# Regrouping the high and low parts of split fp32 products, with weight lows, latent casts and mixing work moved

## The chip, the cores and the metric

The kernel runs on one core of a Trainium2 chip. The metric is the device time of one execution in microseconds. TensorE (PE) multiplies matrices into PSUM, whose eight banks hold 512 fp32 columns each in this kernel; VectorE (DVE), ScalarE (ACT) and GpSimd (POOL) work beside it; SyncE (SP) issues most of the DMAs.

## The reference

Two layers over 512 latent and 256 context tokens (768 in all, six blocks of 128), width 1024, in fp32. Each layer is a half-step SwiGLU FFN, a token mixer, and a second FFN; each of these three is modulated (shift, scale, gate) and closed by a layer norm of the residual sum. The mixer of layer 0 is a chunked gMLP, that of layer 1 is grouped-query attention. The last FFN runs for the latent tokens alone.

```python
def swiglu(h, w_in, w_out):
    g, u = jnp.split(h @ w_in, 2, axis=-1)
    return (jax.nn.silu(g) * u) @ w_out

def ffn_sublayer(x, shift, scale, gate, w_in, w_out, ln_g, ln_b):
    y = swiglu(modulate(x, shift, scale), w_in, w_out)
    return layer_norm(ALPHA * x + 0.5 * gate * y, ln_g, ln_b)

def gmlp_mix(h, w_in, sgu_g, sgu_b, w_s, b_s, w_out):
    b_, t_, _ = h.shape
    u, v = jnp.split(jax.nn.gelu(h @ w_in, approximate=False), 2, axis=-1)
    v = layer_norm(v, sgu_g, sgu_b)
    v = v.reshape(b_, t_ // CHUNK, CHUNK, GMLP_GROUPS, GMLP_HALF // GMLP_GROUPS)
    v = jnp.einsum('gpq,bnqgc->bnpgc', w_s, v) + b_s.T[None, None, :, :, None]
    return (u * v.reshape(b_, t_, GMLP_HALF)) @ w_out

def attend(q, k, v):
    ...
    s = jnp.einsum('bkgqd,bktd->bkgqt', qg, k, preferred_element_type=jnp.float32) * (hd ** -0.5)
    p = jax.nn.softmax(s, axis=-1)
    o = jnp.einsum('bkgqt,bktd->bkgqd', p.astype(v.dtype), v)
```

D_FF is 2816, the gMLP's half width 3072 in 8 groups, chunks have 128 tokens, and there are 8 query heads and 2 key/value heads of 128.

## The kernel before, in words

**Split products.** TensorE multiplies in a shortened fp32 form ("fp32r"). To keep fp32's precision each operand is split into a high part, which ScalarE casts, and a low part, which VectorE makes by subtracting the high part from the operand. A product is then the sum of high by high, high by low and low by high. In `product()` a weight tile `w` (128x512: four pieces of the contraction, `k`) meets a combination `c` of the activations h: twelve matmuls of 128x384, three for each `k`, in the order high-high, high(w)-low(c), low(w)-high(c). `pair_step()` does this for the latent FFN with two times 256 columns. In the gMLP's v a step takes four weights and runs nine matmuls of 128x512 with each, on three PSUM banks, one for each block of tokens; the step's banks are evacuated after the fourth weight. Attention's scores and values are split alike.

**Strassen.** The large products run by a Strassen scheme of two by two blocks, whose right operands are combinations of h (B11, B21, T1 to T4, B22). They are made step by step in the generators `combine()` and `combine_latent()`: VectorE's subtractions `zraw`, `q` and `t`, ScalarE's casts into `comb`, VectorE's low parts of `comb`. `slot()` stands between products: it flushes the pending low parts of weights (`flush()`), takes further weights (`pump()`: each a ScalarE cast now and a VectorE low part that is put off to the next flush), evacuates the finished bank and takes one step of the combining.

**Weights.** SP's queue loads raw tiles of 256 KB into six buffers; some are summed with others for Strassen; the eight `w` buffers hold high and low side by side. The instructions of each engine keep the program's order around all of this, so what is written first is issued first.

**Fillers.** The modulation vectors of later sub-layers are made in between: VectorE multiplies tiles `mraw` of w_mod into `acc` (SCALAR_TENSOR_TENSOR acc<-mraw), and GpSimd reduces them over the partitions. `fill_pair()` issues one filler, or two where only one condition is left (`light`), as in ffn(1,0). GpSimd's queue also carries the activations' spill and return (act<-stage, q<-act).

**Order of the work.** ffn(0,0), gMLP, ffn(0,1), ffn(1,0), attention, latent ffn(1,1). In the gMLP, the spatial mixing of v runs between the products of u: for each of 24 pieces `j` six matmuls of 128x128 (`ps<-zraw,v`), three to a bank in columns 0 to 383, on two banks from a rotation of four (`mix_bank()`); every three pieces, the next group's spatial weight is transposed (`ps<-ident,s`) and summed with a matmul of ones, each in a bank that it takes from the same rotation. VectorE's `S` operations read the banks.

At the end of attention `close()` runs the last block's out-projection in two halves; between them `after(half)` releases four weights and pumps the next four, which are the latent FFN's first. VectorE then makes gate, sum, statistics and `nb`, with which ScalarE normalises `z`.

In the profile nearly every instruction has line 92, that of the wrapper which keeps program order.

Of the kernel before, what the change touches and what calls it, by code (L numbers as in the profile page):

```python
# [13 lines left out]
P = 128  # L14
# [49 lines left out]
OPEN_LAT = [(0, 0), (1, 0), (0, 1), (2, 0), (1, 1), (3, 0), (2, 1), (4, 0), (3, 1), (4, 1)]  # L64

# [31 lines left out]
class Backbone:  # L97
# [707 lines left out]
    def combine(self):  # L805


        sub = lambda out, a, b: self.dve.tensor_tensor(out, a, b, ALU.subtract)
# [80 lines left out]
    def combine_latent(self):  # L889

        N = self.ht // P
        sub = lambda out, a, b: self.dve.tensor_tensor(out, a, b, ALU.subtract)
# [134 lines left out]
    def out_proj(self, acts, l, i, factor, end, prev, gate_at=2):  # L1027
# [9 lines left out]
        for half, order in enumerate(orders):  # L1037
            body = n - CLOSE * half
            for x in range(body):
# [28 lines left out]
                elif residual and x > 2 and (half or x % 2):  # L1068
                    residual.pop(0)()
                    self.fill(int(self.light))  # L1070
                elif half or x < n - 1:
                    self.fill_pair()
                    if prev is None and x % 8 == 3:
                        self.fill()
# [100 lines left out]
    def product(self, ps, name, go_on=False):  # L1175
# [5 lines left out]
        for k in range(4):  # L1181
            s = slice(k * P, k * P + P)
            first, last = not go_on and k == 0, k == 3
            kw = dict(skip_group_check=True) if go_on else {}
            self.mm(ps, w[:, 0, s], c[:, 0, k], first, False, **kw)
            self.mm(ps, w[:, 0, s], c[:, 1, k], False, False, **kw)
            self.mm(ps, w[:, 1, s], c[:, 0, k], False, last, **kw)
# [137 lines left out]
    def pair_step(self, ps, name, go_on, early=None, post=lambda: None):  # L1325

        for x in range(2):
# [5 lines left out]
            for k in range(4):  # L1333
                s = slice(k * P, k * P + P)
                self.mm(o, w[:, 0, s], c[:, 0, k], not go_on and not x and k == 0, False, **kw)
                self.mm(o, w[:, 0, s], c[:, 1, k], False, False, **kw)
                self.mm(o, w[:, 1, s], c[:, 0, k], False, k == 3, **kw)
# [137 lines left out]
    def gmlp_v(self, room, spill, vst):  # L1475
# [43 lines left out]
        def step(x, name, go_on, evacuate):  # L1519
            kw = dict(skip_group_check=True) if go_on else {}  # L1520
            for k in range(4):
# [4 lines left out]
                for t in range(HALF):  # L1526
                    ps, s = sets[x][t], slice(t * P, t * P + P)
                    self.mm(ps, c[:, 0, k, s], w[:, 0], not go_on and k == 0, False, **kw)
                    self.mm(ps, c[:, 0, k, s], w[:, 1], False, False, **kw)
                    self.mm(ps, c[:, 1, k, s], w[:, 0], False, k == 3, **kw)  # L1530
# [86 lines left out]
    def gmlp(self, l, i, nblocks, end, prev):  # L1617
# [30 lines left out]

        def group(g):
# [6 lines left out]
            act.copy(wT, ps[:, 0:P])  # L1656
            yield
            ps = mix_bank()
            self.mm(ps[:, 0:P], self.ones, wT, True, True)
            dve.tensor_copy(r, ps[:, 0:P])  # L1660
# [30 lines left out]
        def spatial(j):  # L1691
# [4 lines left out]
            self.grp_next = next(self.following)  # L1696
            if j % 3 == 2:
                load_ws(j // 3 + 2)
            v = ring[:, j % 4]
            banks = [mix_bank(), mix_bank()]  # L1700
            for b in range(NB):
                o = (b % HALF) * P
                self.mm(banks[b // HALF][:, o : o + P], v[:, b], wT, True, True)
            fetches.append([2, j + 4])
# [162 lines left out]
    def attention(self, l, i, nblocks, end, prev):  # L1867
# [71 lines left out]
        def scores(n):  # L1939
# [4 lines left out]
            for c in (slice(0, 512), slice(512, TOK)):  # L1944
                self.mm(sc[:, c], qh, k[:, 0, c], True, False)
                self.mm(sc[:, c], qh, k[:, 1, c], False, False)
                self.mm(sc[:, c], ql, k[:, 0, c], False, True)
# [29 lines left out]
        def values(pr):  # L1977
# [3 lines left out]
            for t0, t1 in ((0, 3), (3, NB)):  # L1981
                for t in range(t0, t1):
                    ph, pl = [pT[pr % 2][:, x, t] for x in range(2)]
                    self.mm(po, v[:, 0, t], ph, t == 0, False)
                    self.mm(po, v[:, 0, t], pl, False, False)
                    self.mm(po, v[:, 1, t], ph, False, t == NB - 1)
# [96 lines left out]
        def closing(b):  # L2083
# [461 lines left out]
```

## Time and profile before

| | |
|---|---|
| median of 3 runs | 2770.55 us (2768.8 to 2772.38) |
| profiled execution | 2770.93 us |
| its span, first to last instruction | 2769.1 us |
| mean granted TensorE clock | 0.996 |
| busy: TensorE, VectorE, ScalarE, GpSimd | 2716.4, 2139.0, 1377.7, 675.0 us |
| matmuls | 14930 |
| read from and written to HBM | 401.75 and 65.77 MB, 169 GB/s |

Rows of the timeline read: start and length in us, engine, line, operation, tiles written and read, shape, and in brackets the idle time ahead of it and what ended that. The ends of matmuls are modelled, so a matmul's length (about 0.39 us for 512 columns) is longer than the distance from one start to the next; a row of several matmuls shows that distance as the difference between two rows' lengths, divided by the difference of their counts.

### The profile page before, as it was taken

The numbers are of one execution on the slowest core, as the hardware profiler recorded it, in microseconds if no ns is written. First come the engines' busy times: TensorE is split into PE (matmuls) and PEld (weight loads), VectorE is DVE, ScalarE is ACT, GpSimd is POOL, SyncE is SP. The second block draws the span as 40 slices with busy tenths as digits, with TensorE's granted clock in tenths as the row PEclk, the third lists the DMA queues.
The fourth block names the chain that finished last, engine by engine and source line by source line (L and its number), as shares of the span: only waits on it lengthen the run. The fifth ranks groups of instructions, "written<-read, shape, count | busy, mean of one in ns | idle before, by whom it ended". The sixth has DMA issues, their size and how long they took to land.

```text
span 2769.1 us, 42794 instructions
## 1 busy us (share of the span) xinstructions
PE 2716.4 (98%) x14930; PEld 2480.4 (90%) x14930; DVE 2139.0 (77%) x3724; ACT 1377.7 (50%) x2755; POOL 675.0 (24%) x829
## 2 busy tenths in 40 slices
PE   7999999999999999999999999999999999999998
PEld 5999987888899988899998889999888888899987
DVE  6878878487789977687887659788785698787766
ACT  7544433475666632654444246444432666665532
POOL 1003255312122344100325130024342121122121
PEclk9999999999999999999999999999999999999999
DMA  7444566367656674344547534455594524489673
GB/s 236 143 138 139 145 222 220 104 212 233 202 178 190 210 259 139 120 150 142 145 135 236 163 106 145 142 148 142 173 311 146 149 69 87 127 209 216 164 234 133
DMA packets 442896, 468.15 MB, mean 169 GB/s; under 512 B 30840, under 2 KB 323128, under 8 KB 442680
## 3 DMA queue, kind: packets, MB, share of 16 engines
q1 hardware_dynamic: 393592, 343.00, 40.7%
q0 software_dynamic: 49088, 122.42, 15.4%
q8 instruction: 117, 1.92, 0.3%
q14 instruction: 99, 0.81, 0.1%
HBM read 401.75 MB, written 65.77 MB: 169 GB/s over the span
## 4 chain that ended last, share of the span: by engine, by line
PE 57%; DVE 4%; ACT 3%; issue 2%; DMA 2%; POOL 1%; SPq 0%; DVEq 0%; ACTq 0%; POOLq 0%
PE ps L92 56%; DMA raw<-in_ffn_w_in_dram 1%; DVE w L92 1%; PE pp L92 1%; ACT h L763 0%; DVE q L92 0%; ACT z L2443 0%; POOL acc L542 0%; ACT w L92 0%; ACT p L1957 0%; DVE stage L92 0%; DMA mraw<-in_w_mod_dram 0%; DMA raw<-in_gmlp_w_in_dram 0%; DVE z L92 0%; DVE nm L1949 0%
## 5 line engine op out<-in xcount | busy, mean ns | idle before, releaser
L92 PE MATMUL ps<-comb,w 128*128 128x384 f32 (+1 forms) x8400 | 1381.0, 324 | 11.9 <-DVE w L92 3.7
L92 PEld LDWEIGHTS ps<-comb,w 128*128 128x128 f32 x8400 | 1361.0, 189 | 20.1 <-DVE w L92 7.1
L92 PE MATMUL ps<-w,acts 128*128 128x512 f32 (+1 forms) x3792 | 863.8, 389 | 4.7 <-DVE q L92 4.1
L92 PEld LDWEIGHTS ps<-w,acts 128*128 128x128 f32 x3792 | 707.8, 188 | 152.5 <-DVE q L92 4.9
L92 ACT CAST w<-raw 128x512 fp32r<-128x512 f32 x655 | 401.8, 622 | 486.0 <-PE ps L92 369.9
L92 DVE TENSOR_TENSOR w<-raw,w 128x512 fp32r<-128x512 f32 x655 | 455.0, 702 | 240.2 <-ACT w L92 237.8
L542 POOL PARTITION_ALL_REDUCE acc<-acc x224 | 294.2, 1385 | 276.5 <-DVE acc L92 248.5
L92 DVE SCALAR_TENSOR_TENSOR acc<-mraw,cs,acc 128x512 f32<-128x512 f32 x392 | 284.8, 760 | 42.4 <-DMA mraw<-in_w_mod_dram 42.1
L92 ACT COPY q<-ps 128x384 f32<-128x384 f32 (+1 forms) x248 | 122.0, 493 | 266.4 <-PE ps L92 262.6
L92 POOL DMA_DIRECT2D act<-stage x92 | 57.6, 675 | 780.5 <-DVE stage L92 734.3
L92 DVE TENSOR_TENSOR w<-sums,w 128x512 fp32r<-128x512 f32 x278 | 191.3, 696 | 59.4 <-ACT w L92 58.4
L92 POOL DMA_DIRECT2D q<-act x240 | 135.4, 621 | 320.3 <-DVE acts L92 180.0
L92 ACT CAST w<-sums 128x512 fp32r<-128x512 f32 x278 | 171.6, 621 | 57.4 <-DVE sums L92 30.3
L92 DVE TENSOR_TENSOR acts<-q,acts 128x384 fp32r<-128x384 f32 (+2 forms) x278 | 153.0, 589 | 31.2 <-ACT acts L92 31.1
L92 PE MATMUL ps<-w,comb 128*128 128x512 f32 x756 | 173.6, 390 | 1.4 <-ACT ps L92 1.0
L92 ACT CAST acts<-q 128x384 fp32r<-128x384 f32 (+2 forms) x278 | 132.8, 512 | 77.6 <-DMA q<-act 60.2
L92 PEld LDWEIGHTS ps<-w,comb 128*128 128x128 f32 x756 | 141.3, 188 | 32.3 <-ACT ps L92 1.7
L206 POOL TENSOR_TENSOR rs<-ve,mhalf 128x1 f32<-128x1 f32 (+3 forms) x47 | 38.2, 812 | 262.8 <-DVE ve L203 167.2
L92 ACT ACTIVATE q<-q 128x384 f32<-128x384 f32 (+1 forms) x94 | 51.2, 554 | 82.4 <-DVE q L92 82.2
L346 DVE TENSOR_TENSOR sums<-raw 128x512 f32<-128x512 f32 x78 | 55.4, 710 | 31.0 <-DMA raw<-in_gmlp_w_in_dram 18.3
L92 PE MATMUL ps<-w,h 128*128 128x512 f32 x336 | 77.9, 391 | 0.0
L92 ACT COPY ps<-ps 128x384 f32<-128x384 f32 (+1 forms) x60 | 28.5, 475 | 98.1 <-PE ps L92 97.9
(200 smaller groups left out, 2485.6 us busy)
## 6 DMA issues: line engine op xcount, KB each, us to landing
raw<-in_ffn_w_in_dram SPq DMA_DIRECT2D x420, 256.0 KB
mraw<-in_w_mod_dram SPq DMA_DIRECT2D x256, 256.0 KB
raw<-in_ffn_w_out_dram SPq DMA_DIRECT2D x176, 256.0 KB
q<-act POOLq DMA_DIRECT2D x224, 192.0 KB, 4.3
raw<-in_gmlp_w_in_dram SPq DMA_DIRECT2D x132, 256.0 KB
act<-stage POOLq DMA_DIRECT2D x76, 384.0 KB, 3.2
zhat<-z POOLq DMA_DIRECT2D x26, 512.0 KB, 3.0
raw<-in_gmlp_w_out_dram SPq DMA_DIRECT2D x48, 256.0 KB
```

The source lines that it names most:

```text
L92: return self.tc.keep_in_program_order(f(*args, **kwargs))
L206: self.last_rstd = self.nc.gpsimd.tensor_tensor(rs, ve, self.mhalf[:, 0:1].to_broadcast([P, n]), ALU.pow).ins
L346: dve.tensor_tensor(s1, u1, u2, ALU.add)
L542: nc.gpsimd.partition_all_reduce(part, part, P, bass_isa.ReduceOp.add)
```

## The change

It has five parts, each of them a change of order; the number of instructions of each kind stays the same.

1. In `product()`, `pair_step()`, the gMLP's v, attention's scores and its values, all high-high matmuls come first, then those with the low part of the activations, then those with the low part of the weights. The low part of `w` is wanted by the ninth of twelve matmuls, before by the third (in v by the seventh of nine, before by the second); that of `c` by the fifth, before by the second.
2. In `combine()` and `combine_latent()` the function `sub` flushes the pending weight lows right behind each subtraction.
3. In the out-projection of a light FFN (ffn(1,0)) the pair of fillers after the first step of the first half is left out there, and comes a step later.
4. In the spatial mixing the group's transposition and ones matmul use columns 384 to 511 of the second bank of the piece that has just been multiplied, and come behind its six matmuls.
5. At the end of attention `after()` also pumps behind the second half, with low parts put into free slots of VectorE's order at once (`slots`), so that four more weights are cast and lowered before the last block is closed.

```diff
+PARTS = (0, 0), (0, 1), (1, 0)
...
     def combine(self):
-        sub = lambda out, a, b: self.dve.tensor_tensor(out, a, b, ALU.subtract)
+        def sub(out, a, b):
+            self.dve.tensor_tensor(out, a, b, ALU.subtract)
+            self.flush()
...
-                elif half or x < n - 1:
+                elif half or x < n - 1 and (x or not self.light):
                     self.fill_pair()
...
         c = self.comb[name]
-        for k in range(4):
-            s = slice(k * P, k * P + P)
-            first, last = not go_on and k == 0, k == 3
-            kw = dict(skip_group_check=True) if go_on else {}
-            self.mm(ps, w[:, 0, s], c[:, 0, k], first, False, **kw)
-            self.mm(ps, w[:, 0, s], c[:, 1, k], False, False, **kw)
-            self.mm(ps, w[:, 1, s], c[:, 0, k], False, last, **kw)
+        kw = dict(skip_group_check=True) if go_on else {}
+        for n, (x, y) in enumerate(PARTS):
+            for k in range(4):
+                s = slice(k * P, k * P + P)
+                first, last = not go_on and n == 0 and k == 0, n == 2 and k == 3
+                self.mm(ps, w[:, x, s], c[:, y, k], first, last, **kw)
...
-                for t in range(HALF):
-                    ps, s = sets[x][t], slice(t * P, t * P + P)
-                    self.mm(ps, c[:, 0, k, s], w[:, 0], not go_on and k == 0, False, **kw)
-                    self.mm(ps, c[:, 0, k, s], w[:, 1], False, False, **kw)
-                    self.mm(ps, c[:, 1, k, s], w[:, 0], False, k == 3, **kw)
+                for n, (i, j) in enumerate(PARTS):
+                    for t in range(HALF):
+                        s = slice(t * P, t * P + P)
+                        first, last = not go_on and n == 0 and k == 0, n == 2 and k == 3
+                        self.mm(sets[x][t], c[:, j, k, s], w[:, i], first, last, **kw)
...
+        beside = []
+        def spare():
+            return beside.pop() if beside else mix_bank()[:, 0:P]
...
-            ps = mix_bank()
-            self.tp(ps[:, 0:P], ws_raw.pop(g))
+            ps = spare()
+            self.tp(ps, ws_raw.pop(g))
...
-            self.grp_next = next(self.following)
...
             for b in range(NB):
                 o = (b % HALF) * P
                 self.mm(banks[b // HALF][:, o : o + P], v[:, b], wT, True, True)
+            beside[:] = [banks[1][:, HT : HT + P]]
+            self.grp_next = next(self.following)
...
                 def after(half):
                     self.release(4)
-                    if not half:
-                        self.pump()
+                    self.slots = bool(half)
+                    self.pump()
+                    self.slots = False
```

What this does to the order of the instructions is shown at three places. In the rows, numbers tell tiles apart.

VectorE at the opening of ffn(1,0): `w` rows are weight lows, `zraw`, `q` and `t4` the subtractions, `comb` the low part of a combination. Before:

```order
L92 TENSOR_TENSOR zraw_16424<-z_14840,h32_16097 128x512
L92 TENSOR_TENSOR q_16426<-z_14840,zraw_16424 128x512
L92 TENSOR_TENSOR w_16418<-raw_16017,w_16418 128x512
L92 TENSOR_TENSOR t4_16449<-h32_16097,q_16426 128x512
L92 TENSOR_TENSOR comb_16423<-q_16426,comb_16423 128x4x128
L92 TENSOR_SCALAR z_14840<-ps_16457,modA_16089,modB_16090 128x128 x4
L92 TENSOR_TENSOR w_16444<-raw_16045,w_16444 128x512
```

After:

```order
L94 TENSOR_TENSOR zraw_16410<-z_14826,h32_16083 128x512
L94 TENSOR_TENSOR w_16404<-raw_16003,w_16404 128x512
L94 TENSOR_TENSOR q_16413<-z_14826,zraw_16410 128x512
L94 TENSOR_TENSOR t4_16435<-h32_16083,q_16413 128x512
L94 TENSOR_TENSOR w_16430<-raw_16031,w_16430 128x512
L94 TENSOR_TENSOR comb_16409<-q_16413,comb_16409 128x4x128
```

The first low part moved ahead of q, the second ahead of comb's low part and of the four TENSOR_SCALAR.

TensorE where the spatial mixing meets the preparation of a group. Before:

```order
L92 MATMUL ps_7247<-comb_6029,w_7191 128x384 x12
L92 MATMUL ps_7411<-zraw_7295,v_5589 128x128 x3
L92 MATMUL ps_7412<-zraw_7295,v_5589 128x128 x3
L92 MATMUL ps_7423<-ident_69,s512_7240 128x128
L92 MATMUL ps_7427<-zraw_7295,v_5589 128x128 x3
L92 MATMUL ps_7428<-zraw_7295,v_5589 128x128 x3
L92 MATMUL ps_7436<-comb_5305,w_7200 128x384 x12
```

After:

```order
L94 MATMUL ps_7247<-comb_6029,w_7191 128x384 x12
L94 MATMUL ps_7410<-zraw_7295,v_5589 128x128 x3
L94 MATMUL ps_7411<-zraw_7295,v_5589 128x128 x3
L94 MATMUL ps_7423<-zraw_7295,v_5589 128x128 x3
L94 MATMUL ps_7424<-zraw_7295,v_5589 128x128 x3
L94 MATMUL ps_7424<-ident_69,s512_7240 128x128
L94 MATMUL ps_7435<-comb_5305,w_7200 128x384 x12
```

The transposition stands behind the second piece, and writes the bank that this piece has written.

VectorE where the last block of attention is closed (gate into `q`, sum into `z`, statistics, `ve1`, `nb`). Before:

```order
L176 TENSOR_TENSOR w_23941<-raw_23503,w_23941 128x512
L988 SCALAR_TENSOR_TENSOR q_23963<-ps_23913,gate_22895 128x512
L999 TENSOR_TENSOR z_23697<-z_23697,q_23963 128x512
L1004 BN_STATS st_23702<-z_23697 128x6
L965 BN_AGGR mv_23967<-st_23702 128x2
L203 TENSOR_SCALAR ve1_23969<-mv_23967 128x1
L970 SCALAR_TENSOR_TENSOR nb_23973<-mv_23967,rs1_23970 128x1
```

After:

```order
L178 TENSOR_TENSOR w_23927<-raw_23489,w_23927 128x512
L998 SCALAR_TENSOR_TENSOR q_23965<-ps_23899,gate_22881 128x512
L178 TENSOR_TENSOR w_23944<-raw_23567,w_23944 128x512
L1009 TENSOR_TENSOR z_23683<-z_23683,q_23965 128x512
L178 TENSOR_TENSOR w_23948<-raw_23572,w_23948 128x512
L1014 BN_STATS st_23688<-z_23683 128x6
L178 TENSOR_TENSOR w_23952<-raw_23915,w_23952 128x512
L975 BN_AGGR mv_23969<-st_23688 128x2
L178 TENSOR_TENSOR w_23956<-raw_23920,w_23956 128x512
L205 TENSOR_SCALAR ve1_23971<-mv_23969 128x1
L980 SCALAR_TENSOR_TENSOR nb_23975<-mv_23969,rs1_23972 128x1
```

Four weight lows, which stood behind `nb` before, stand between its operations.

More of the change, by code (lines that the diff above doesn't have):

```diff
@@ L891, in combine_latent, with sub @@
         N = self.ht // P
-        sub = lambda out, a, b: self.dve.tensor_tensor(out, a, b, ALU.subtract)
+        def sub(out, a, b):
+            self.dve.tensor_tensor(out, a, b, ALU.subtract)
+            self.flush()
         cut = lambda t: t[:, :].rearrange("p (k t) -> p k t", t=P)
@@ L1332, in pair_step @@
             c, o = self.comb[name], ps[:, x * self.ht : x * self.ht + self.ht]
[L1333 to L1337, printed above, removed]
+            for n, (i, j) in enumerate(PARTS):
+                for k in range(4):
+                    s = slice(k * P, k * P + P)
+                    first, last = not go_on and not x and n == 0 and k == 0, n == 2 and k == 3
+                    self.mm(o, w[:, i, s], c[:, j, k], first, last, **kw)
         self.slot(post, 4, 0, early)
@@ L1525, in step @@
                 c = self.comb[name]
-                for t in range(HALF):
-                    ps, s = sets[x][t], slice(t * P, t * P + P)
-                    self.mm(ps, c[:, 0, k, s], w[:, 0], not go_on and k == 0, False, **kw)
-                    self.mm(ps, c[:, 0, k, s], w[:, 1], False, False, **kw)
-                    self.mm(ps, c[:, 1, k, s], w[:, 0], False, k == 3, **kw)
+                for n, (i, j) in enumerate(PARTS):
+                    for t in range(HALF):
+                        s = slice(t * P, t * P + P)
+                        first, last = not go_on and n == 0 and k == 0, n == 2 and k == 3
+                        self.mm(sets[x][t], c[:, j, k, s], w[:, i], first, last, **kw)
                 if k == 3:
@@ L1652, in group @@
             yield
-            ps = mix_bank()
-            self.tp(ps[:, 0:P], ws_raw.pop(g))
+            ps = spare()
+            self.tp(ps, ws_raw.pop(g))
             wT = self.zplace()[:, 0:P]
-            act.copy(wT, ps[:, 0:P])
+            act.copy(wT, ps)
             yield
-            ps = mix_bank()
-            self.mm(ps[:, 0:P], self.ones, wT, True, True)
-            dve.tensor_copy(r, ps[:, 0:P])
+            ps = spare()
+            self.mm(ps, self.ones, wT, True, True)
+            dve.tensor_copy(r, ps)
             yield wT, r, bs
@@ L1695, in spatial @@
             wT, r, bs = self.grp
-            self.grp_next = next(self.following)
-            if j % 3 == 2:
-                load_ws(j // 3 + 2)
             v = ring[:, j % 4]
@@ L1703, in spatial @@
                 self.mm(banks[b // HALF][:, o : o + P], v[:, b], wT, True, True)
+            beside[:] = [banks[1][:, HT : HT + P]]
+            self.grp_next = next(self.following)
+            if j % 3 == 2:
+                load_ws(j // 3 + 2)
             fetches.append([2, j + 4])
@@ L1943, in scores @@
             sc = self.pair()
[L1944 to L1947, printed above, removed]
+            for m, (x, y) in enumerate(PARTS):
+                for c in (slice(0, 512), slice(512, TOK)):
+                    self.mm(sc[:, c], (qh, ql)[x], k[:, y, c], m == 0, m == 2)
             nm = self.sm([1], "nm")
@@ L1981, in values @@
             for t0, t1 in ((0, 3), (3, NB)):
[L1982 to L1986, printed above, removed]
+                for n, (x, y) in enumerate(PARTS):
+                    for t in range(t0, t1):
+                        self.mm(po, v[:, y, t], pT[pr % 2][:, x, t], n == 0 and t == 0, n == 2 and t == NB - 1)
                 if t1 < NB:
```

## The prediction

> **What bounds the kernel now.** I read the page's busy times first, then who TensorE waits for, then TensorE's timeline wherever a wait stood.
>
> ```profile
> span 2769.1 us, 42794 instructions
> PE 2716.4 (98%) x14930; PEld 2480.4 (90%) x14930; DVE 2139.0 (77%) x3724; ACT 1377.7 (50%) x2755; POOL 675.0 (24%) x829
> PE ps L92 <- DVE w L176: 4.4, 11, 1.0
> PE ps L92 <- DVE w L92: 4.0, 9, 0.7
> ```
>
> TensorE is busy for 98% of the span, so the kernel is TensorE's stream plus 52.7 us of its gaps. The change leaves the number of matmuls as it is; it can win only at gaps, and at the slow stretches that follow some of them. The two last rows are the gaps that a weight's low part ends: 8.4 us in all, much of it at the start, in matmuls outside the products.
>
> **The openings of the two light FFNs, ffn(0,1) and ffn(1,0).** TensorE, VectorE and ScalarE at the second of them, and the weight loads' wait from 1100 to 1400 us:
>
> ```profile
> 1667.52 2.70 PE L92 MATMUL ps<-comb,w 128*128 128x384 f32 x14
> 1670.76 2.35 PE L92 MATMUL ps<-comb,w 128*128 128x384 f32 x12 [0.55 <-DVE w L92]
> 1673.84 0.44 PE L92 MATMUL ps<-comb,w 128*128 128x384 f32 x1 [0.73 <-DVE w L92]
> 1670.02 0.68 DVE L92 TENSOR_TENSOR w<-raw,w 128x512 fp32r<-128x512 f32 x1
> 1670.66 0.62 ACT L92 CAST w<-raw 128x512 fp32r<-128x512 f32 x1
> PEld ps L92 <- DVE w L92: 1.9, 2, 1.0
> ```
>
> Fourteen matmuls take 2.70 us and twelve 2.35, so one costs 0.175. After fourteen from 1667.52 the next was due at 1669.97 and came at 1670.76, 0.8 late; twelve from there were due to end at 1672.86, and the next came at 1673.84, 1.0 late. Both times two matmuls of a product had run and the third wanted the low part. In the new order the low part is wanted by the ninth, six matmuls (1.05 us) later, and VectorE makes it one subtraction (0.6 us) earlier. That covers both lags. What is late next is the second weight's cast: ScalarE's cast of h's combination waits for q, which now stands behind the low part, so the cast at 1670.66 moves 0.6 later and ends near 1671.9, where its product is due at about 1671.7: 0.2 lost of 1.8. From 1100 to 1400 the last row shows the same two waits at ffn(0,1) (they are the only ones there). Gain 1.65 twice, **+3.3** (0 if VectorE is late all the same, up to 3.6).
>
> **Two single starts.** The first product of the first FFN, and the first weight of the gMLP's v; the last row is the group of all v's matmuls:
>
> ```profile
> 48.62 0.62 PE L92 MATMUL ps<-comb,w 128*128 128x384 f32 x2 [1.89 <-ACT w L175]
> 49.69 3.52 PE L92 MATMUL ps<-comb,w 128*128 128x384 f32 x10 [0.45 <-DVE w L176]
> 562.64 0.49 PE L92 MATMUL ps<-w,comb 128*128 128x512 f32 x1 [0.19 <-ACT w L92]
> 563.37 2.12 PE L92 MATMUL ps<-w,comb 128*128 128x512 f32 x8 [0.23 <-DVE w L92]
> L92 PE MATMUL ps<-w,comb 128*128 128x512 f32 x756 | 173.6, 390 | 1.4 <-ACT ps L92 1.0
> ```
>
> At 48.62 two matmuls should take 0.35 and took 1.07: 0.7 goes; the wait for ScalarE ahead stays, and so does the half-speed stretch behind it (ten matmuls in 3.52). At 562.64 one matmul took 0.73 where 0.23 is due: 0.5 goes. **+1.2** (0.5 to 1.7).
>
> **Spatial mixing.** TensorE at its two long waits, and a stretch of the span with the granted clock in the next to last column group (time, TensorE busy, clock, DMA share, GB/s):
>
> ```profile
> 748.82 0.83 PE L92 MATMUL ps<-zraw,v 128*128 128x128 f32 x6
> 751.61 0.91 PE L92 MATMUL ps<-zraw,v 128*128 128x128 f32 x6 [1.95 <-DVE S L92]
> 752.76:756.17 3.41, 3.41 (x13) 0.50 0.59 168
> 750.84 1.14 DVE L92 SCALAR_TENSOR_TENSOR S<-ps,sguT,s 128x384 f32<-128x384 f32 x2
> 929.34 0.83 PE L92 MATMUL ps<-zraw,v 128*128 128x128 f32 x6
> 931.61 0.91 PE L92 MATMUL ps<-zraw,v 128*128 128x128 f32 x6 [1.43 <-DVE S L92]
> ```
>
> Here the group's transposition or its ones matmul takes a bank of its own out of the rotation of four, so a second spatial step comes back to a bank that the step before it still has in use, and waits for VectorE. With that work in the spare columns each step takes exactly two banks and meets those of two steps ago. Six matmuls from 748.82 end their issue near 749.5; the next came at 751.61: 2.1. From 929.34: 1.6. The first wait is followed by 3.41 us at half the granted clock, in which 1.7 us of matmuls are lost. **+5.4** (3.5 if the half-clock stretch stays or falls elsewhere; 5.5).
>
> The trace granted half the clock after an idle time of 1.95 us. The Trainium skill, "TensorE: Matmul & The Clock Gate", section "Why this matters for your kernels", warns only of idle gaps above about 3 us. By that rule the 1.7 us here would have another cause and stay, and the new 2 us waits below could not halve the clock; the sum would be 2761.5 instead of 2760.7. The row decides.
>
> **The gMLP's v, where the new order costs.** A step takes four weights, and with each runs nine matmuls on the same three banks; 756 / 36 = 21 steps. Before, three matmuls run on each bank in turn; after, every matmul changes the bank. TensorE, ScalarE's evacuations, the weight loads, and a stretch with the clock:
>
> ```profile
> 687.62 3.79 PE L92 MATMUL ps<-w,comb 128*128 128x512 f32 x16
> 692.41 1.88 PE L92 MATMUL ps<-w,comb 128*128 128x512 f32 x7 [1.00 <-ACT ps L92]
> 691.76 0.59 ACT L92 COPY ps<-first 128x512 f32<-128x512 f32 x1 [0.83 <-DVE q L92]
> 649.66 0.59 ACT L92 COPY ps<-v 128x512 f32<-128x512 f32 x1
> 650.30 0.76 PEld L92 LDWEIGHTS ps<-w,comb 128*128 128x128 f32 x4 [0.25 <-ACT ps L92]
> 687.00:690.40 3.40, 3.40 (x17) 1.00 0.70 260
> ```
>
> One matmul costs (3.79 - 0.39) / 15 = 0.227 us. The step's third bank is written first by the third matmul now, by the seventh before: 0.91 us earlier. At 692.41 TensorE waited for just that bank, whose preset ended at 692.35; it would wait 0.91 longer, about 2.0. At 650.30 the bank's copy ended at 650.25, just in time; now 0.9 is lost. Together **-1.8** (0 if ScalarE's copies come earlier, -3.6 if the first bank, finished four matmuls later, delays them as much again). A wait of 2.0 is as long as the one that cost 1.7 us of half clock at 749, while the wait of 1.43 has no such stretch behind it; at even odds **-0.9**.
>
> The Trainium skill, same page, section "A second HAM failure mode: psum-queue depth-cycling", tells of a kernel with 512 columns whose cycling through banks left short idle times and an oscillating clock. Here sixteen matmuls with five changes of bank run without a gap at clock 1.00, which speaks against it; it stands below as a rival.
>
> **The light out-projection of ffn(1,0).**
>
> ```profile
> 1991.38 4.83 PE L92 MATMUL ps<-w,acts 128*128 128x512 f32 x13 [3.35 <-DVE q L92]
> 1987.37 0.75 DVE L92 SCALAR_TENSOR_TENSOR acc<-mraw,cs,acc 128x512 f32<-128x512 f32 x1 [4.08 <-DMA mraw<-in_w_mod_dram]
> ```
>
> The longest gap is made by a modulation filler that holds VectorE for 4.08 us until its weight lands. It is issued at the end of the FFN's first phase; the pair that the change takes out comes behind it, after the first out-projection step, and is made a step later, with its all-reduces on GpSimd, ahead of which some of the activations' transfers now go. So **0**: the cover of the moved pair is TensorE's stream with no wait there. Bounds: two fillers of 0.75 in front of VectorE's work, -1.5; and if the stall went, +3.4 and the 1.7 of half clock that a gap of this length brings.
>
> **The end of attention and the latent opening.** TensorE, VectorE and ScalarE:
>
> ```profile
> 2402.58 2.90 PE L92 MATMUL ps<-comb,w 128*128 128x256 f32 x22 [1.01 <-DVE w L176]
> 2409.98 1.70 PE L92 MATMUL ps<-comb,w 128*128 128x256 f32 x12 [0.77 <-ACT pieces L92]
> 2413.29 0.51 PE L92 MATMUL ps<-comb,w 128*128 128x256 f32 x2 [1.61 <-ACT w L92]
> 2414.11 1.77 PE L92 MATMUL ps<-comb,w 128*128 128x256 f32 x10 [0.32 <-DVE w L92]
> 2417.24 2.95 PE L92 MATMUL ps<-comb,w 128*128 128x256 f32 x18
> 2401.84 2.49 DVE L176 TENSOR_TENSOR w<-raw,w 128x512 fp32r<-128x512 f32 x4
> 2407.70 1.24 ACT L2443 ACTIVATE z<-z,nb,rs 128x1024 f32<-128x1024 f32 x1 [5.12 <-DVE nb L970]
> 2409.36 0.57 ACT L92 COPY pieces<-ps 128x512 f32<-128x512 f32 x1
> ```
>
> The first low part is ready at 2402.5; it is wanted six matmuls of 0.12 later, 0.7 gained. Then the price: four more low parts (0.62 each, 2.5) stand between VectorE's gate, sum, statistics and nb. Some of it fills latency, so nb and the ACTIVATE behind it come about 2 us later, near 2409.6. The copy of the pieces, now without a cast ahead of it, ends near 2411.5, not at 2409.93, and TensorE, early by 0.7, waits about 3 us instead of 0.77. But the waits of 1.61 and 0.32 fall away, since the four weights are ready: two products (24 x 0.12 = 2.9) and the transposes (about 1) bring the product of 2417.24 to about 2415.5, of which I leave 0.7 for a half-clock stretch in that 3 us wait. With ScalarE's four casts hidden in its 5.12 us of idleness, **+1.0** (-0.6 to +3).
>
> **The latent FFN, 2440 to 2530**, the weight loads' waits there:
>
> ```profile
> PEld ps L92 <- DVE w L92: 2.8, 8, 0.6
> PEld ps L92 <- ACT w L92: 1.4, 2, 1.2
> ```
>
> Eight times the third matmul waited for a low part; six matmuls of 0.12 more time and an earlier place cover each (0.6 at most). The wait for ScalarE's casts stays. As transfers pace some weights there, I take two thirds: **+2.0** (0.5 to 3.2).
>
> Scores and values of attention change only the order in which ready operands are used: 0, within 1 us.
>
> **Sum.** 3.3 + 1.2 + 5.4 - 1.8 - 0.9 + 0 + 1.0 + 2.0 = 10.2. The profiled execution took 2770.9 (1.8 outside its span); the median of the runs is 2770.55, 0.4 less, and they spread by 1.8 each way, about one half-clock stretch. 2770.9 - 10.2 = **2760.7 us**. No change and a change are told apart here from 0.2%, 5.5 us.
>
> **Rivals.**
> - The stall at 1987 goes too (a filler moved is a transfer asked for at another time): 2760.7 - 5.1 = 2755.6. Against it: its filler stands ahead of all that moved. Chance 0.14.
> - The waits move on instead of away: VectorE, not the order of parts, is the limit in the openings and the latent FFN, so 3.3 and 2.0 are not won and the latent opening loses 1: 2760.7 + 7.3 = 2768.0. For it: at 1670 VectorE ran back to back; against it: six matmuls of slack exceed each wait. 0.22, of which 0.04 below 2765.
> - Slower: the v steps. All 21 need the third bank 0.91 earlier; I count two that are late. If the evacuations, paced by VectorE, run late in more, each costs 0.91, and 2.6 where its wait grows to the 2 us that bring a half-clock stretch. Seven more of these give 2760.7 + 18.2 = 2778.9; from six more on (15.6 us) the change is slower by over 0.2%. Against it: before, one step alone made TensorE wait for more than a trace of time (1.0 of the group's 1.4 us). 0.07, of which 0.06 above the bound.
> - The clock oscillates through all of v: 756 x 0.227 = 172 us run at half clock, about 2930. 0.01. The skill's section on cycling is what speaks for it.
>
> **How the numbers follow.** The forecast, 2757 to 2765, has 0.56. Faster by over 0.2% (below 2765): 0.56 + 0.14 + 0.04 = 0.74. Slower: 0.06 + 0.01 = 0.07. Within: 0.19. The range for 8 in 10 takes in the forecast, most of the first rival and most of the second: 2752 to 2769.
>
> **What would show it.** Right: no DVE w wait at 1162, 1165, 1670, 1673 and 563; no S wait in mixing and clock 1.00 after 749; a wait for ACT ps of about 2 us near 690 and a new one of 0.9 near 649; one wait of 3 us near 2409 for pieces; the 3.35 us gap before the out-projection as it was. Wrong: a spread of small waits in v, new waits for comb's low parts, which VectorE makes later now, or matmuls slower by the new order; 1 ns on each of the 8400 of ps<-comb,w would be 8.4 us.

## The result

The changed kernel is slower: 2784.55 us (median of 5, 2778.3 to 2787.87) against 2770.55 (median of 5), a ratio of 1.0046 with a 95% interval of 1.0029 to 1.0062. The forecast was 2760.7, 10 us faster, and a range of 2752 to 2769; the rival with v's banks as the one mechanism (2778.9) names one of the two causes, the smaller one.

The profiled execution took 2785.96 us. Four of TensorE's waits before (lines marked L92), then page and waits after (L94):

```profile
PE ps L92 <- DVE S L92: 3.4, 2, 1.9
PE ps L92 <- ACT w L92: 2.8, 3, 1.6
PE ps L92 <- ACT ps L92: 1.0, 1, 1.0
PE ps L92 <- ACT pieces L92: 0.8, 1, 0.8
span 2784.1 us, 42785 instructions
PE 2721.7 (98%) x14930; PEld 2482.3 (89%) x14930; DVE 2138.8 (77%) x3724; ACT 1377.8 (49%) x2755; POOL 679.0 (24%) x829
PE ps L94 <- DVE w L94: 4.1, 3, 2.4
PE ps L94 <- ACT w L94: 3.6, 7, 1.2
PE ps L94 <- ACT pieces L94: 3.5, 3, 2.8
PE ps L94 <- ACT zraw L94: 3.3, 2, 1.7
PE ps L94 <- ACT ps L94: 3.0, 2, 2.6
```

The matmuls are the same 14930. The waits for VectorE's S (3.4 us before) are gone. The waits for ScalarE have grown: for its casts `w` from 2.8 to 3.6 us, for its copies to `pieces` from 0.8 to 3.5, for the banks (`ps`) from 1.0 to 3.0, and 3.3 us for its copies to `zraw` are new. Of the 4.1 us for VectorE's w, 3.9 now lie in the latent out-projection.

Since both programs issue 14930 matmuls, the start of TensorE's n-th one can be compared between two traces. The table gives how many us each stage lost against the one trace of before (minus is gained); the last column is the difference at the last matmul. "Same again" is a kernel whose instructions are those of before (see the third set of runs), so its row shows what two executions of one program differ by.

| stage (us in the trace of before) | 3-541 | v 541-732 | mixing, out 732-962 | ffn(0,1) 962-1213 | ffn(1,0) 1213-1740 | its out-projection -2014 | attention -2386 | latent opening -2439 | latent FFN -2557 | latent out -2758 | all |
|---|---|---|---|---|---|---|---|---|---|---|---|
| changed | 5.8 | 6.6 | -4.3 | 2.1 | 2.4 | -0.1 | 0.2 | -0.6 | -1.8 | 4.8 | 15.0 |
| changed, no flush | 3.7 | 2.3 | -3.8 | 0.5 | 0.2 | 0.4 | 0.2 | -0.8 | -4.1 | 0.6 | -0.8 |
| late flush | 1.4 | 6.0 | -3.1 | -0.2 | 0.1 | 0.0 | 0.8 | -0.9 | -3.0 | 4.7 | 5.9 |
| flush alone | 3.7 | 4.5 | -3.0 | 2.4 | 2.3 | -0.3 | 0.0 | 0.8 | -0.2 | 0.8 | 11.0 |
| new order in v alone | 2.0 | 4.4 | -1.6 | 0.0 | 0.0 | -1.6 | 0.0 | 0.0 | -2.1 | 0.0 | 1.3 |
| new order in the products alone | 1.8 | 0.8 | -3.5 | -0.5 | -0.4 | 0.0 | 0.4 | -1.0 | -1.0 | 1.7 | -1.7 |
| mixing's columns alone | 0.4 | 2.9 | -4.9 | 0.1 | 0.6 | -1.8 | 0.0 | 0.0 | -2.6 | 1.6 | -3.8 |
| same again | 2.9 | 0.2 | -2.3 | 0.0 | 0.0 | -0.3 | 0.0 | 0.0 | -4.5 | 0.0 | -4.0 |
| no fillers in the last pass | 3.3 | -0.3 | -2.5 | 0.0 | 0.0 | -5.4 | 0.2 | 0.0 | -4.5 | 0.0 | -9.3 |

Two things are to be read here. The openings repeat well (0.0 in the repeat of before, 0.6 at most, either way, in all kernels without the flush), so 2.1 and 2.4 are losses of the change. The start, mixing and the latent FFN differ by 2 to 4.5 us between executions of one program: there a single trace carries less than the prediction drew from it.

**The opening of ffn(0,1), where two low waits were to go.** TensorE, VectorE and ScalarE of the changed kernel:

```profile
1177.90 8.92 PE L94 MATMUL ps<-comb,w 128*128 128x384 f32 x48 [0.23 <-ACT w L94]
1187.30 6.54 PE L94 MATMUL ps<-comb,w 128*128 128x384 f32 x36 [0.48 <-ACT acc L94]
1195.50 1.83 PE L94 MATMUL ps<-comb,w 128*128 128x384 f32 x9 [1.66 <-ACT zraw L94]
1177.88 0.69 DVE L94 TENSOR_TENSOR w<-raw,w 128x512 fp32r<-128x512 f32 x1 [0.48 <-ACT w L94]
1184.06 0.69 DVE L94 TENSOR_TENSOR w<-raw,w 128x512 fp32r<-128x512 f32 x1 [0.48 <-ACT w L94]
1190.00 0.69 DVE L94 TENSOR_TENSOR w<-raw,w 128x512 fp32r<-128x512 f32 x1 [0.61 <-ACT w L94]
1191.39 1.23 ACT L94 CAST comb<-z 128x512 fp32r<-128x512 f32 x2 [1.03 <-DVE z L94]
1194.97 0.48 ACT L94 COPY zraw<-ps 128x384 f32<-128x384 f32 x1
```

The waits for DVE w are gone. But now VectorE stands still ahead of the lows, because their casts have not ended yet; the subtraction behind them (z) comes late, ScalarE's cast of z waits 1.03 us for it, and the copy that frees a bank, queued some operations behind that cast, starts at 1194.97. TensorE waits 1.66 us for that bank, 20 us behind the place where the wait was removed.

**The gMLP's v.** TensorE and VectorE, the granted clock from 658 to 664 (the number after the five engines), and the spatial mixing:

```profile
605.88 4.40 PE L94 MATMUL ps<-w,comb 128*128 128x512 f32 x18 [0.68 <-ACT w L94]
611.04 2.37 PE L94 MATMUL ps<-w,comb 128*128 128x512 f32 x9 [0.75 <-ACT w L94]
614.59 1.66 PE L94 MATMUL ps<-w,comb 128*128 128x512 f32 x6 [1.19 <-ACT w L94]
602.69 0.69 DVE L94 TENSOR_TENSOR w<-raw,w 128x512 fp32r<-128x512 f32 x1 [1.75 <-ACT w L94]
658.30 0.51 PE L94 MATMUL ps<-w,comb 128*128 128x512 f32 x1 [0.34 <-ACT ps L94]
661.45 3.10 PE L94 MATMUL ps<-w,comb 128*128 128x512 f32 x8 [2.65 <-ACT ps L94]
658.00:664.00 6.00, 3.05 (x9) 2.22 (x10) 5.86 (x11) 5.07 (x11) 2.30 (x5) 0.86 0.61 214
759.94 2.84 PE L94 MATMUL ps<-zraw,v 128*128 128x128 f32 x24
762.62 0.27 PE L94 MATMUL ps<-ident,s 128*128 128x128 f32 x1
```

Three new waits for casts near 610 follow a low that held VectorE for 1.75 us. At 661.45 TensorE wanted the step's third bank and waited 2.65 us, with a half-clock stretch behind it. In mixing, the 24 matmuls, of which six had to wait 1.95 us before, are one run without a gap, and the transposition follows them.

**The out-projection and the latent opening** look as forecast:

```profile
2003.73 2.50 PE L94 MATMUL ps<-w,acts 128*128 128x512 f32 x5 [3.17 <-DVE q L94]
2415.17 2.18 PE L94 MATMUL ps<-comb,w 128*128 128x256 f32 x16 [0.28 <-DVE w L178]
2423.90 4.35 PE L94 MATMUL ps<-comb,w 128*128 128x256 f32 x23 [2.82 <-ACT pieces L94]
2422.14 1.24 ACT L2456 ACTIVATE z<-z,nb,rs 128x1024 f32<-128x1024 f32 x1 [2.42 <-DVE nb L980]
```

The gap at the out-projection stayed. In the latent opening the first wait fell from 1.01 to 0.28, the one for pieces grew from 0.77 to 2.82, and the waits of 1.61 and 0.32 that stood behind it are gone.

### The profile page after: what moved, and what is told of

It reads as the page before. It is cut to its first block, busy times and chain, and to the rows that moved or that the text cites. A ratio compares the mean times of both kernels' runs of the same rounds, so it can differ in the third digit from the quotient of the medians.

```text
span 2784.1 us, 42785 instructions
## 1 busy us (share of the span) xinstructions
PE 2721.7 (98%) x14930; PEld 2482.3 (89%) x14930; DVE 2138.8 (77%) x3724; ACT 1377.8 (49%) x2755; POOL 679.0 (24%) x829
## 4 chain that ended last, share of the span: by engine, by line
PE 73%; issue 6%; DVE 6%; DMA 5%; ACT 5%; POOL 3%; SPq 0%; DVEq 0%; ACTq 0%; POOLq 0%
PE ps L94 72%; POOL acc L544 2%; DMA raw<-in_ffn_w_in_dram 2%; DMA mraw<-in_w_mod_dram 2%; DVE w L94 2%; ACT w L94 1%; PE pp L94 1%; ACT h L765 1%; DMA raw<-in_w_mod_dram 1%; DVE z L94 1%; DMA q<-act 1%; DVE q L94 1%; ACT z L2456 0%; DVE acc L94 0%; SPq L94 0%
## 5 line engine op out<-in xcount | busy, mean ns | idle before, releaser
L94 PE MATMUL ps<-comb,w 128*128 128x384 f32 (+1 forms) x8400 | 1381.3, 324 | 14.8 <-ACT pieces L94 3.5
L94 PEld LDWEIGHTS ps<-comb,w 128*128 128x128 f32 x8400 | 1360.6, 189 | 23.8 <-ACT q L94 5.0
L94 PE MATMUL ps<-w,acts 128*128 128x512 f32 (+1 forms) x3792 | 864.7, 389 | 9.1 <-DVE w L94 3.9
L94 PEld LDWEIGHTS ps<-w,acts 128*128 128x128 f32 x3792 | 707.6, 188 | 158.0 <-DVE w L94 5.1
L94 ACT CAST w<-raw 128x512 fp32r<-128x512 f32 x651 | 399.5, 621 | 493.3 <-PE ps L94 370.3
L94 DVE TENSOR_TENSOR w<-raw,w 128x512 fp32r<-128x512 f32 x651 | 452.0, 701 | 246.5 <-ACT w L94 244.4
L94 DVE SCALAR_TENSOR_TENSOR acc<-mraw,cs,acc 128x512 f32<-128x512 f32 x392 | 285.1, 760 | 44.3 <-DMA mraw<-in_w_mod_dram 44.0
L94 ACT COPY q<-ps 128x384 f32<-128x384 f32 (+1 forms) x248 | 122.5, 495 | 265.5 <-PE ps L94 262.7
L94 POOL DMA_DIRECT2D act<-stage x92 | 59.2, 710 | 786.8 <-DVE stage L94 738.2
L94 DVE TENSOR_TENSOR w<-sums,w 128x512 fp32r<-128x512 f32 x278 | 191.1, 695 | 52.7 <-ACT w L94 51.4
L94 POOL DMA_DIRECT2D q<-act x240 | 136.3, 626 | 313.8 <-DVE acts L94 182.5
L94 ACT CAST w<-sums 128x512 fp32r<-128x512 f32 x278 | 171.4, 621 | 58.2 <-DVE sums L94 30.8
L94 PE MATMUL ps<-w,comb 128*128 128x512 f32 x756 | 175.8, 393 | 5.8 <-ACT ps L94 3.0
L94 DVE TENSOR_TENSOR acts<-q,acts 128x384 fp32r<-128x384 f32 (+2 forms) x278 | 152.6, 587 | 35.0 <-ACT acts L94 34.9
L94 PEld LDWEIGHTS ps<-w,comb 128*128 128x128 f32 x756 | 142.5, 189 | 37.7 <-ACT w L94 4.5
L94 ACT CAST acts<-q 128x384 fp32r<-128x384 f32 (+2 forms) x278 | 132.2, 512 | 76.2 <-DMA q<-act 58.8
L94 ACT ACTIVATE q<-q 128x384 f32<-128x384 f32 (+1 forms) x94 | 51.3, 554 | 83.1 <-DVE q L94 83.1
L94 PE MATMUL ps<-w,h 128*128 128x512 f32 x336 | 77.9, 391 | 0.0
L178 DVE TENSOR_TENSOR w<-raw,w 128x512 fp32r<-128x512 f32 x93 | 61.6, 686 | 20.7 <-ACT w L177 20.1
```

Source lines behind the costliest of these rows:

```text
L94: return self.tc.keep_in_program_order(f(*args, **kwargs))
L178: self.lows.append((key, lambda: self.dve.tensor_tensor(lo, src, hi.bitcast(F32), ALU.subtract)))
```

## The experiments

Times are medians of 11 or 12 runs (5 for the flush alone), beside 27 to 35 runs of the kernel before on the same chip; its medians there were 2768.4 to 2769.9. The sets ran on three chips, so kernels of different sets are compared by their ratios to before.

### First set: the flush and the order in v

In the changed kernel, the flush undone:

```diff
         def sub(out, a, b):
             self.dve.tensor_tensor(out, a, b, ALU.subtract)
-            self.flush()
```

> The changed kernel with one part undone: weight lows are no longer flushed behind each subtraction of the combinations. Flush theory (a low put early into VectorE's queue waits there for its ScalarE cast, VectorE's next subtractions come late, ScalarE's copies behind them too, and TensorE waits for banks): the start loses no 5 us, v about 1 instead of 6.6, the two light openings gain 1.6 each instead of losing 2.1 and 2.4, mixing and the latent FFN keep their gains; about 2762, up to 2767 if the waits of 1.7 and 2.5 us at the end of the latent out-projection stay. Order theory (high parts first is what costs, in v's banks and in the openings): no more than 2 us won, about 2782.

2772.87 us, ratio to before 1.0013 (1.0005 to 1.0022). That is 11.7 us less than the changed kernel by the medians, and 9.1 by the two ratios: 9 to 12 us of the 14 are the flush. The flush theory holds, though not to 2762: the forecast gains are not there either.

The same three lines added to the kernel before, and nothing else:

> The kernel before with the flush behind each subtraction alone. Flush theory: the start loses 3 to 5, v about 3, the openings 1 to 2 each since the products still want a low at the third matmul; about 2780. Order theory: within 2 us of before, about 2770.

2779.08, ratio 1.0033 (1.0021 to 1.0044): 9.2 us slower, as the flush theory had it.

The changed kernel without the flush and with v's loop as before:

> The changed kernel without the flush and with the old order of parts in the gMLP's v. Flush theory: within 2 us of the kernel without the flush, 2761 or so, with 0 to 1.8 won in v. Order theory: 5 to 6.6 us faster than with the new order in v.

2769.13, ratio 0.9999 (0.999 to 1.0007). v's order costs 3.7; between the two theories' numbers, and its price has the size of the prediction's term. What is left of the change gains nothing measurable.

v's new loop alone in the kernel before:

> The kernel before with the new order of parts in the gMLP's v alone. Prediction's term: 0.5 won at the start of v, 1.8 to 2.7 lost at two steps, about 2772. Order theory: 6 us lost in v with waits for ScalarE's casts and evacuations near 604 and 657, about 2777. Flush theory: no waits for casts near 604 to 613.

2772.89, ratio 1.0013 (1.0004 to 1.0022): 3.0 slower. In its trace TensorE waits 0.3 us for casts near 604 to 613, as in the kernel without the flush (0.3); with the flush alone it is 0.9, with both 2.6. So those waits need the flush, and the two parts together make them longer.

How the flush works shows in VectorE's waits for casts between 1150 and 1230 us (between 1160 and 1240 for the changed kernel): in total, times, longest. In this order before, the changed kernel, the flush alone, the changed kernel without the flush (and with the same row the late flush of the second set):

```profile
DVE w L92 <- ACT w L92: 3.8, 5, 1.3
DVE w L94 <- ACT w L94: 4.5, 9, 1.1
DVE w L94 <- ACT w L94: 3.4, 8, 0.6
DVE w L94 <- ACT w L94: 1.4, 3, 0.7
```

The totals alone say little, since before has 3.8 us without any flush. What matters is where the waits stand. The rows of L94 are the flush alone, those of L92 are before; both lists end with the last two subtractions `z`:

```profile
1166.39 0.69 DVE L94 TENSOR_TENSOR zraw<-z,h 128x512 f32<-128x512 f32 x1 [1.09 <-ACT z L94]
1169.49 0.69 DVE L94 TENSOR_TENSOR w<-raw,w 128x512 fp32r<-128x512 f32 x1 [0.48 <-ACT w L94]
1175.08 0.69 DVE L94 TENSOR_TENSOR w<-raw,w 128x512 fp32r<-128x512 f32 x1 [0.48 <-ACT w L94]
1181.27 0.69 DVE L94 TENSOR_TENSOR w<-raw,w 128x512 fp32r<-128x512 f32 x1 [0.48 <-ACT w L94]
1184.10 0.69 DVE L94 TENSOR_TENSOR w<-raw,w 128x512 fp32r<-128x512 f32 x1 [0.33 <-ACT w L94]
1187.20 0.69 DVE L94 TENSOR_TENSOR w<-raw,w 128x512 fp32r<-128x512 f32 x1 [0.60 <-ACT w L94]
1187.81 1.29 DVE L94 TENSOR_TENSOR z<-z 128x512 f32<-128x512 f32 x2
1161.09 0.69 DVE L92 TENSOR_TENSOR zraw<-z,h 128x512 f32<-128x512 f32 x1 [1.09 <-ACT z L92]
1179.49 1.28 DVE L92 TENSOR_TENSOR z<-z 128x512 f32<-128x512 f32 x2
```

From the opening's first subtraction to these two VectorE takes 21.4 us with the flush and 18.4 before. With the flush five waits for the weights' casts, 2.4 us in all, fall into this stretch. Before there are none of them, only 0.3 us for another cast. One low more ahead of the subtractions (0.6) makes most of the rest. TensorE loses 2.4 us in this stage.

### Second set: a later flush, and three parts without it

```diff
+        seen = []
         def sub(out, a, b):
             self.dve.tensor_tensor(out, a, b, ALU.subtract)
-            self.flush()
+            lows, self.lows = self.lows, []
+            for low in lows:
+                if any(low is x for x in seen):
+                    low[1]()
+                else:
+                    self.lows.append(low)
+            seen[:] = self.lows
```

> The changed kernel, but a weight low is issued behind a subtraction only if it was already pending at the subtraction before: its ScalarE cast has one VectorE operation more of time. Theory that the low waits for its cast in VectorE's queue: the idle times of 0.48 us ahead of VectorE's lows in the light openings, the wait of 1.8 us for ScalarE's zraw copy and v's waits for casts near 604 go for the most part; 2773 to 2776. Theory that the mere place of the low ahead of q and of comb's low part is what costs: 2780 to 2784 as in the changed kernel.

2772.27, ratio 1.0016 (1.0006 to 1.0026): equal to no flush at all (1.0013) within the noise; the wait for the zraw copy falls from 1.7 to 0.6 us. By the traces, though, this edit undoes most of the flush: set against VectorE's other operations, it issues 12 of the 1080 weight lows earlier than the kernel without the flush does and 7 later, while the full flush issues 53 earlier. So its time alone does not tell the wait for the cast from the mere place of the low. Its rows do so in the opening:

```profile
1167.95 0.69 DVE L94 TENSOR_TENSOR comb<-q,comb 128x512 fp32r<-128x512 f32 x1
1168.55 0.68 DVE L94 TENSOR_TENSOR w<-raw,w 128x512 fp32r<-128x512 f32 x1
```

The low that waited 0.48 us behind the subtraction t stands one operation later, behind comb's low part, without a wait. Three lows stand earlier in this opening than in the kernel without the flush, none waits for its cast, and the stage loses nothing (-0.2 in the table). In the openings, then, it is the wait for the cast that costs; for the other stages this is not shown. (Its v has the new order still, and loses 6.0.)

The mixing's spare columns alone (part 4 of the change):

> The kernel before with the mixing's spare columns alone. Prediction's term: both waits for VectorE's S (2.0 and 1.5) gone, 3.5 to 5.4 won, 2765 to 2766.5. Rival: the waits move on to VectorE's q at 883 and into small gaps at the mixing's matmuls, and the half clock at 752 in the first profile was chance; 1 to 2 won, about 2768.5.

2768.13, ratio 0.9998 (0.9989 to 1.0007). The two S waits are gone from its trace; the 0.6 us won lie inside the interval. The rival was right about the half clock: the repeat of before waited 1.82 us at this place and kept the full clock. So did the kernel with the new order in the products alone, which has the old mixing; its wait, and the granted clock behind it (after the five engines):

```profile
753.46 0.91 PE L94 MATMUL ps<-zraw,v 128*128 128x128 f32 x6 [1.69 <-DVE S L94]
754.40:757.80 3.40, 3.40 (x21) 3.40 (x20) 3.23 (x8) 1.30 (x4) 0.73 (x2) 1.00 0.52 131
```

The new order in `product()` and `pair_step()` alone:

> The kernel before with the new order of parts in the FFNs' products alone (product and pair_step). Prediction's terms: 3.3 won in the openings, 2.0 in the latent FFN, 0.7 at the start; 2764. Rival, waits move on: the low waits go, and 20 us later TensorE waits as long for ScalarE's copies to acc and q, since VectorE and ScalarE pace the opening; 2 to 3 won in the latent FFN alone, 2767.5 to 2768.

2769.18, ratio 0.9996 (0.9987 to 1.0005). TensorE at the opening of ffn(0,1) there:

```profile
1165.29 0.97 PE L94 MATMUL ps<-comb,w 128*128 128x384 f32 x4 [0.48 <-DVE w L94]
1186.12 26.17 PE L94 MATMUL ps<-comb,w 128*128 128x384 f32 x149 [0.23 <-ACT acc L94]
```

Of the two low waits one is left, at the ninth matmul; 20 us later TensorE waits for a copy of ScalarE's. The opening as a whole gains 0.5.

Mixing, `pair_step()` and the latent casts together:

> The kernel before with three parts: the mixing's spare columns, the new order in the latent FFN's products, and the four latent casts moved up. From the traces so far: 1 to 2, 2 and 0.8 won, about 2765.5 and the fastest yet if the order in the 128x384 products brings nothing; if that order does bring its 3.3, it is no faster than the same with it, 2769.

2769.45, ratio 0.9998 (0.9989 to 1.0007): no gain. The traces with the latent casts moved up gain 0.6 to 0.9 us in the column "latent opening", too little to show in a time. They all have the new order in `pair_step()` too, and that order without the casts gained 1.0 in its one trace, where the half-clock stretch near 2415 did not come. So what the casts give by themselves is not shown.

### Third set: v's banks, and a filler edit that did nothing

v's new order only for the second and third weight of a step:

```diff
+                order = [(t, n) for t in range(HALF) for n in (0, 2, 1)]
+                if k in (1, 2):
+                    order = [(t, n) for n in range(3) for t in range(HALF)]
```

> The kernel before with the new order of parts in the gMLP's v only for the second and third of a step's four weights, so that a step's banks are first written and last finished as before. Bank theory (the third bank wanted 0.91 us earlier and the first finished later is what costs the 3 us of the new order in v): no cost, 2769 to 2770. Theory that the order itself is slower (a change of bank at every matmul, lows and highs in another order): half of the 3 us, about 2771.

2766.46, ratio 0.9995 (0.9986 to 1.0003): no cost. TensorE near 650 with v's new order throughout, and with it in the middle of a step alone:

```profile
654.40 7.79 PE L94 MATMUL ps<-w,comb 128*128 128x512 f32 x21 [2.65 <-ACT ps L94]
651.82 8.47 PE L94 MATMUL ps<-w,comb 128*128 128x512 f32 x36 [1.24 <-ACT ps L94]
```

So the cost lies in the first and last nine matmuls of a step, where the banks are taken up and given back; a change of bank at every matmul in the eighteen between costs nothing. Whether the third bank, wanted earlier, or the first, finished later, costs more is not separated. The waits for banks in one trace say less than the time: over all of v they add up to 2.7 to 3.8 us in the four traces with the new order throughout, and to 0.5 to 3.3 in the eleven with the old. A half-clock stretch follows in three of the four and in two of the eleven. On average that makes 1.4 us of waits and 1.8 us of half clock, of the size of the 3.0 and 3.7 measured.

Then the gap at the light out-projection was to be removed by leaving out its fillers, in three kernels:

```diff
-            self.tile_strassen(..., int(f >= OPENED) * (2 + f % 2))
+            self.tile_strassen(..., int(f >= OPENED and not (self.light and f == FF - 1)) * (2 + f % 2))
```

> The kernel before without the modulation fillers of the last pass of a light FFN's first phase (they are made later, in the out-projection). Theory that the filler's wait for mraw makes the gap of 3.4 us and its half-clock stretch at 1988: both go, 4 to 5 us won, about 2764.5. Rival, the wait moves on with the fillers into the out-projection, where VectorE's lows stand behind them: 0 to 2 won, 2768 or more.

> The changed kernel without the flush, with the old order in v, and without the fillers of the last pass before the light out-projection. If gains add: 2769.1 less 4 to 5, about 2764.5, as the fillers alone; if latent FFN, openings and mixing bring nothing of their own it is equal to the kernel with that edit alone.

> Mixing's spare columns, the new order in the latent FFN's products, the latent casts moved up, and no fillers in the last pass before the light out-projection. If gains add: 2769.4 less 4 to 5, about 2765; a candidate for the fastest version.

`light` is not yet set in that pass, so the edit moved no instruction. The three are repeats: of before (2768.01 beside 2768.52, ratio 0.9999), of the changed kernel without the flush and v's order (2767.58, first 2769.13), and of mixing, pairs and casts (2767.93, first 2769.45). They show what the measurement repeats to, 1.5 us, and the first gives the table its row "same again". The gap at the out-projection is 3.00 us in the first and only 1.58 in the third, where it was 3.21 the first time.

### Fourth set: the gap at the out-projection

Open was by then whether a wait of TensorE that is taken away shows in the time at all. Now the condition is met:

```diff
+            self.tile_strassen(..., int(f >= OPENED and not (l == 1 and i == 0 and f == FF - 1)) * (2 + f % 2))
```

> The kernel before without the modulation fillers in the last pass of the first phase of ffn(1,0); this time the condition is met (the earlier edit's never was, so that its kernel was the one before). Theory that the filler's wait for mraw makes the 3.4 us gap near 1988 and its half-clock stretch: both go, 2768.5 less 4 to 5, about 2764. Rival, the wait moves with the fillers into the out-projection: 0 to 2 won.

2763.56, ratio 0.9984 (0.9976 to 0.9993): 4.9 us faster. With the next kernel, equal to it within the noise, it is the fastest version here. Its out-projection starts without a gap:

```profile
1984.88 7.46 PE L94 MATMUL ps<-w,acts 128*128 128x512 f32 x32
```

The stage gains 5.4 in the table (5.1 against the repeat of before), where the prediction had priced this gap at 5.1 (3.4 and 1.7 of half clock).

> The changed kernel without the flush, with the old order in v, and without those fillers. If the remaining parts gain nothing measurable: equal to the kernel with the fillers alone left out, about 2764. If they gain 2 or more: 2762 or less.

2763.76, ratio 0.9983 (0.9974 to 0.9992).

> The kernel before without those fillers, with the mixing's spare columns, and with the new order in v for the second and third weight of a step alone. About 2763 if the parts add (4.5, 0.6 and up to 1 won), a candidate for the fastest version; 2764 if only the fillers count.

2764.44, ratio 0.9987 (0.9978 to 0.9995). Neither adds anything measurable to the fillers' 4.9.

## Why the prediction was wrong

- **Part 2, the flush: this step failed.** "VectorE makes it one subtraction (0.6 us) earlier" was counted as help, and the second weight's later cast was priced at 0.2 us. The prediction followed that cast to TensorE only. VectorE needs it as well: the flush puts the second low behind the subtraction t, where VectorE waits for this cast (0.48 us at 1177.88), and comb's low part, the next subtractions, ScalarE's casts of them and its copies of banks all come later. At the latent opening the prediction did follow the queue behind the added lows. Measured: 9 to 12 us. By the table's rows with and without the flush, 3.8 to 4.7 of it stand in the two light openings together, 4.3 in v (where traces without flush or new order differ by 3 us among themselves) and 2.3 to 4.3 in the latent FFN. Only in the openings do the rows show the whole way from the cast to TensorE.
- **The openings, +3.3.** Without the flush they lost 0.5 and 0.2 in one trace and gained 0.5 and 0.4 in another. The second rival, "the waits move on", describes it: the low is still late for one ninth matmul (0.48), and ScalarE's copies are late next. VectorE worked there without a pause but for 0.3 us from 1161 to 1191 before, so it paces the opening whichever matmul wants the low.
- **v, -1.8 and -0.9 for a half clock, +0.5 at its start.** Right in size and mechanism: -3.0 alone and -3.7 taken away, by waits for banks and half clock. The place was 650 rather than 691: the wait of 1.0 at 691 is absent from the repeat of before, while the one near 650 is there with the old order too, 0.5 to 2.2 in all other traces, and the trace of before had just escaped it ("the bank's copy ended at 650.25, just in time").
- **Mixing, +5.4.** The mechanism was right, the size was not: both S waits went, but the 1.7 of half clock belonged to that one execution. Five others with the same wait (1.5 to 1.8), the repeat of before among them, kept the full clock. Against that repeat the stage gained 2.6 in the trace of the spare columns alone; the time gained 0.6, inside its noise.
- **The latent FFN, +2.0.** Not of the change: the kernel of before itself ran this stretch 4.5 us faster when it was profiled again. Its weight loads' waits for lows, 2.8 us in the one trace, were 1.2 in the other.
- **The start, +0.7.** It differs by 2 to 3 us between executions; nothing can be read there.
- **The latent opening, +1.0, the out-projection, 0.** Right in number: 0.6 to 0.9, with the wait of 2.8 for the pieces and the falling waits behind it as described, though the new order alone gained 1.0 in its trace, so the four casts are not shown to be the reason. Before, a half-clock stretch stood there already (from 2415.05, not counted in the prediction); after, one stands behind the wait for the pieces, so the two cancel. And a gain of 0.1 at the out-projection, with the gap untouched. Of its price of 5.1 the gap's length returned; its 1.7 of half clock did not come in two traces, after 3.31 and 3.08 us.
- **Not foreseen**: 4.8 us in the latent out-projection, for lows behind a filler that waits for its transfer. They are 0 to 4.7 in the other kernels, without any order in it, so I do not count them to the change; their cause, the transfers' pace, stays open.

Of the forecast gains of 12.9 us, 4.4 stood in one execution (half clock, latent FFN, start) and 3.3 moved on to ScalarE and VectorE. The other 5 or so (mixing's waits, the latent casts, v's start) show in the traces in part, but the parts left without flush and banks give ratios of 0.9999 and 1.0001: how much of these 5 us comes back elsewhere, and where, is not settled. Taken out one after the other, flush and banks are worth 11.7 and 3.7 us, and the rest gains 0.75; these are steps of one chain and must add up to the whole. Put singly into the kernel before, the two cost 9.2 and 3.0, 12.2 of the 14.0 between the medians.

## What to carry to other kernels

To issue an operation earlier in an in-order queue is no gain unless its input is there by then: look up the end of the producer (here ScalarE's cast) for the new place, and follow the queue behind it to the bank that it frees. Before waits of one profile are summed up, a second profile of the same kernel tells which of them return; here the gap at the out-projection did (3.0 to 3.7 us in 13 of 14 traces that have its fillers, 1.6 in one), the half clock in mixing and most of the latent FFN's waits did not. And the gap was worth its length and the half clock behind it where its cause was removed (5.4 in the trace, 4.9 in the time), while the waits bridged by looser needs in the openings came back 20 us later, as the engines behind them were as busy as before.

## What the hardware showed

Whether a gap halves the clock is partly chance. In mixing, idle times of 1.49 to 1.84 us passed at full clock in five traces, 1.95 in one did not. In v, 2.65 us was followed by a half-clock stretch in all three traces that had it. Ahead of the out-projection, gaps of 3.0 to 3.7 us were followed by one in eleven traces, and in two they were not. One of the two, v's new loop alone, with the granted clock behind the gap:

```profile
1996.24 0.96 PE L94 MATMUL ps<-w,acts 128*128 128x512 f32 x3 [3.31 <-DVE q L94]
1996.24:2003.00 6.76, 6.76 (x30) 5.60 (x31) 6.51 (x11) 4.28 (x9) 4.28 (x6) 1.00 1.01 364
```

The Trainium skill ("TensorE: Matmul & The Clock Gate", "Part 1: The HAM clock gate") describes a window of 3413 ns that runs freely of the kernel. That agrees with the traces: the stretches last 3.41 us or twice that, and the one in mixing did not come again in the repeat of before, while those near 1992 and 2415 did. Its advice (section "Why this matters for your kernels") to avoid gaps above about 3 us is too coarse here: 1.95 us was enough once, and 3.31 us passed once without a slower clock.
